# Cutting one product of each down chunk into two products of 256 columns

## The chip, the cores and the metric

The kernel runs on one core of one Trainium2 chip. The metric is the device time of one execution in microseconds (us). Before the change the median of 3 runs is 964.23 us (964.13 to 964.59).

## The reference

Two transformer-like blocks run one after the other on 256 tokens of width 1024, in fp32. Cut to what matters here:

```
x = x + rms_norm(mixer(rms_norm(x)))                        # attention of two kinds and a delta rule
u = conv3(rms_norm(x) @ w_up) + b                           # 1024 -> 2 * 2816
x = x + rms_norm((gelu(gate) * up) @ w_down)                # 2816 -> 1024
h = h + (u * spatial_gate(layernorm(v))) @ a_w_out          # 2048 -> 1024
h = h + square(relu(rms_norm(h) @ mlp_w1[0])) @ mlp_w2[0]   # 1024 -> 4096 -> 1024
h = h + latent_attention(rms_norm(h))
h = h + square(relu(rms_norm(h) @ mlp_w1[1])) @ mlp_w2[1]
out = rms_norm(h)
```

Four of these lines end in a product that comes "down" from a wide hidden vector to 1024 columns: `w_down`, `a_w_out`, and `mlp_w2` twice. The change touches these four.

## The kernel before, in words

**Products.** Every large fp32 product is done as three products of rounded operands (`fp32r`): each operand is split into a high part and a low part (`s0h`, `s0l` for a weight, `aT0h`, `aT0l` for an activation), and `mm3` (L456) issues high by high, high by low, low by high into the same PSUM bank. The first two of the three have the same stationary operand.

**Up and down.** `updown` (L553) runs each of the four stages. The weights come in chunks. An up chunk gives 256 hidden columns of all 256 tokens: `fm` (L462) does 16 groups of three products of 256 columns, with the weight as the stationary operand and the tokens as the moving one, into a bank named `r_fm`. After some work on ScalarE (ACT) and VectorE (DVE) the result is split into `aT`. A down chunk multiplies `aT` by 256 rows of the down weight: `down` (L486) goes over the two halves of the 1024 output columns, and `tm` (L469) over two blocks of 128 rows, each with three products of 512 columns, with `aT` as the stationary operand and the weight as the moving one. It is called for both blocks of 128 tokens (L599, L600), so a down chunk is 2 x 2 x 2 x 3 = 24 products of 512 columns, into four accumulators named `r_acc`. Up and down chunks alternate, the down chunk being 4 blocks behind the up chunk (`LAG`); in the first of the four stages two up chunks stand between two down chunks. The last 4 down chunks of a stage (`TAIL`) take another path for the second token block (`last_downs`, L620).

**Weights.** SyncE's queue (SP) loads each half chunk into one of four `raw` buffers (L324). ACT rounds it into a slot (`s2h<-raw`) and DVE subtracts (`s2l<-raw,s2h`). There are 4 to 6 slots; a slot is free when the last product that reads it is done. A `raw` buffer is free when DVE has read it, and the load after waits for that.

**Order.** The instruction order is not written out by hand. Threads (Python generators) offer their next instruction, and `run_threads` (L249) always takes the thread whose instruction would start first by the model in `Estimate` (L76); starts within 0.02 us are settled by rank, and a thread of rank 10 or more is put back by 0.3 us. Every instruction is one such choice, and a thread that comes to a free slot or a new event does so when its turn is taken. The model charges a product of n columns n/2400 us and 0.0023 us (L99). On the chip each engine then takes its own instructions strictly in the order that came out.

**Between the stages.** After the second stage, `latent_setup` (L1368) loads constants through the same SP queue, among them `inv_freq` into the tile `vm`, from which the thread `angles` (L1325) computes on DVE.

Of the kernel before, what the change touches and what calls it, by code (L numbers as in the profile page):

```python
# [21 lines left out]
TAIL = 4  # L22
# [22 lines left out]
def updown_plan(n, per=1):  # L45

    ev, nd = [], n // per
    for i in range(n):
        ev.append(("up", i))
        j = (i + 1) // per - 1 - LAG  # L50
        if (i + 1) % per == 0 and j >= 0:
            ev.append(("down", j))
    return ev + [("down", j) for j in range(nd - LAG, nd)]


def weight_plan():
    def stage(up, down, n, per=1):
        return [(up if k == "up" else down, i) for k, i in updown_plan(n, per)]

    seq = [("w_v", 0), ("w_v", 1)]  # L60
    seq += PROJ
    seq += [("w_z", 0), ("w_z", 1)]
    seq += [("w_out", i) for i in range(4)]
    seq += stage("w_up", "w_down", 22, 2)
    seq += [("a_v", i) for i in range(8)]
    seq += stage("a_u", "a_w_out", 8)
    seq += stage("w1_0", "w2_0", 16)
    seq += [("kv_a", 0), ("kv_a", 1), ("q_a", 0), ("q_a", 1)]
    seq += [("kv_b", 1), ("q_bp", 0), ("kv_b", 0), ("q_bn", 0), ("q_bn", 1)]
    seq += [("b_w_o", i) for i in range(4)]  # L70
    seq += stage("w1_1", "w2_1", 16)
    return seq
# [125 lines left out]
class Kernel:  # L198
# [254 lines left out]
            yield from self.T.transpose(dst[:, b * P:(b + 1) * P], src[:, b * P:(b + 1) * P], self.ident)  # L453


    def mm3(self, o, lh, ll, rh, rl, first, last):  # L456
        T = self.T
        yield from T.matmul(o, lh, rh, start=first, stop=False)
        yield from T.matmul(o, lh, rl, start=False, stop=False)
        yield from T.matmul(o, ll, rh, start=False, stop=last)  # L460

    def fm(self, o, w, c0, xT, nk):  # L462

# [2 lines left out]
            yield from self.mm3(o, w[0][:, k, c0:c0 + P], w[1][:, k, c0:c0 + P], xT[0][:, k, :], xT[1][:, k, :],  # L466
                     k == 0, k == nk - 1)

    def tm(self, o, w, xT, t, ks, k0=0, c0=0, n=None, first=True, last=True, ev=None):  # L469

        n = n or w[0].shape[2]
        ts = slice(t * P, (t + 1) * P)
        for i, k in enumerate(ks):
            yield from self.block_ready(w, k)
            if ev and (k0 + k) % 4 == 0:
                yield self.on((ev, t, (k0 + k) // 4))
            yield from self.mm3(o, xT[0][:, k0 + k, ts], xT[1][:, k0 + k, ts], w[0][:, k, c0:c0 + n], w[1][:, k, c0:c0 + n],
                     first and i == 0, last and i == len(ks) - 1)

    def new_acc(self, t):  # L480
        acc = []
# [1 line left out]
            acc.append((yield from self.bank("acc%d" % t)))  # L483
        return acc

    def down(self, acc, w, aT, t, k0, first, last):  # L486
        last = last if isinstance(last, tuple) else (last, last)
        for h in range(2):
            yield from self.tm(acc[h], w, aT, t, (0, 1), k0=k0, c0=h * 512, n=512, first=first, last=last[h])
            if last[h]:  # L490
                self.set(("sum", acc[h].name, 512 * h), acc[h])

# [60 lines left out]
    def updown(self, names, n, per, pool, block, aT, tail, stagger, gains=(), final=False):  # L553

        S, xT, nd = self.S, self.hT, n // per
        acc, st, last = None, {}, []

        def first(c):
            o = yield from self.bank("tp", st[0, c], st[1, c])
            for b in range(2):  # L560
                for t in range(2):
                    yield from self.T.transpose(o[:, b * 256 + t * P:b * 256 + (t + 1) * P], st[t, c][:, b * P:(b + 1) * P],
                                     self.ident)
            yield from block(c, o)

        if stagger:
            ws = []
            for t in range(2):
                for c in range(stagger):
                    if len(ws) <= c:  # L570
                        ws.append((yield from self.chunk(names[0], c)))
                    o = (yield from self.bank("fm"))[:, :256]
                    yield from self.tm(o, ws[c].view(8), xT, t, range(8), ev=names[0])
                    st[t, c] = self.tile(pool, [P, 256], "tmst", bufs=2 * stagger)
                    self.spawn(1, self.copy_out(st[t, c], o))
                    if t:
                        self.free(ws[c])
                        self.spawn(1, first(c))
        else:
            yield self.on((names[0], 0), (names[0], 1))  # L580
        for kind, i in updown_plan(n, per):
            if kind == "up":
                if stagger and i < stagger:
                    continue
                c = yield from self.chunk(names[0], i)
                o = yield from self.up(c.view(8), xT)
                self.free(c)
                self.spawn(1, block(i, o))
                if i == n // 2:
                    self.g = [self.gain(g) for g in gains]  # L590
                continue
            if acc is None:
                acc = [[], []]
                for t in range(2):
                    acc[t] = yield from self.new_acc(t)
            c = yield from self.chunk(names[1], i)
            yield self.on((names[0], "block", i))
            if i < nd - TAIL:
                yield from self.down(acc[0], c.view(2), aT[i], 0, 0, i == 0, False)  # L599
                yield from self.down(acc[1], c.view(2), aT[i], 1, 0, i == 0, (False, final and i == nd - TAIL - 1))  # L600
                self.free(c)
                self.rel(aT[i][0])
            else:
                yield from self.down(acc[0], c.view(2), aT[i], 0, 0, i == 0, i == nd - 1)
                last.append((i, c))
        for t in range(2):
            tail(t, acc[t])
        items = [(c, aT[i], 0) for i, c in last]
        if not final:
            yield from self.last_downs([(acc[1][h], HALVES[h]) for h in range(2)], items, False)  # L610
            return

        for _ in range(2):
            acc[1].append((yield from self.bank("fm")))
        self.set(("sum", "banks"))
        yield from self.last_downs([(acc[1][0], HALVES[0])], items, False)
        for q in range(2):
            yield from self.last_downs([(acc[1][2 + q][:, :256], slice(512 + 256 * q, 768 + 256 * q))], items, True)
# [1010 lines left out]
```

## Time and profile before

| | before |
|---|---|
| median of 3 runs | 964.23 us (964.13 to 964.59) |
| the profiled execution, its time | 963.24 us |
| the profiled execution, its span | 961.5 us |
| mean granted TensorE clock | 0.992 |
| TensorE (PE) busy | 939.2 us, 98% |
| VectorE busy | 648.4 us, 67% |
| ScalarE busy | 515.0 us, 54% |
| instructions | 16153, of them 6475 products and 6475 weight loads |

The profiled execution has 1.74 us more in its time than in its span. All instructions are issued from one helper line, L177, so groups are told apart by the tiles they write and read: `out<-in`, for a product the moving operand first and the stationary one second. A product's row begins when it enters the array and ends with its modelled drain, so rows of successive products overlap, and the distance of two starts is what a product costs in a stream.

### The profile page before, as it was taken

Reading aid. Unit: us, or ns where it says so; the run is one execution under the profiler, and the core shown is the slowest. Engines: PE = TensorE matmul, PEld = TensorE weight load, DVE = VectorE, ACT = ScalarE, POOL = GpSimd, SP = SyncE. Lnnn points to the kernel's source line nnn. Section 1 sums busy time; section 2 is a strip of 40 time slices with the busy share of each in tenths; the row PEclk is TensorE's granted clock in tenths of the full one; section 3 lists DMA queues with packets and bytes.
Section 4 is the critical chain, followed back from the end, with each engine's and each line's share of the span. In section 5 each row is a group of like instructions: output and inputs, shape, how many; then the busy total and the mean of one; then the engine's idle time right before and its main releaser. Section 6 shows DMA issues by size and latency. Waiting matters only on the chain.

```text
span 961.5 us, 16153 instructions
## 1 busy us (share of the span) xinstructions
PE 939.2 (98%) x6475; PEld 863.1 (90%) x6475; DVE 648.4 (67%) x1027; ACT 515.0 (54%) x853; POOL 24.9 (3%) x38
## 2 busy tenths in 40 slices
PE   7999999999999999999998999999999999999997
PEld 6899878899999989999988999998889899999986
DVE  5687776889687757697557765554678687555533
ACT  5664565767566546535445644444557575444421
POOL 0000000000000001000000000000110000000000
PEclk8999999999999999999999999999999999999999
DMA  7732432746777637727645776564345377566511
GB/s 230 252 111 89 132 110 88 223 132 197 254 227 233 201 113 287 244 88 259 193 133 152 244 226 192 192 194 148 96 149 161 111 231 240 186 202 194 193 47 44
DMA packets 48891, 168.22 MB, mean 175 GB/s; under 512 B 6448, under 2 KB 7088, under 8 KB 48560
## 3 DMA queue, kind: packets, MB, share of 16 engines
q1 hardware_dynamic: 48816, 167.19, 54.5%
q8 instruction: 51, 0.84, 0.4%
q14 instruction: 24, 0.20, 0.1%
HBM read 166.12 MB, written 1.05 MB: 174 GB/s over the span
## 4 chain that ended last, share of the span: by engine, by line
PE 90%; DVE 3%; ACT 2%; DMA 2%; issue 1%; SPq 1%; POOL 0%; POOLq 0%; DVEq 0%; ACTq 0%
PE r_fm L177 47%; PE r_acc L177 38%; PE r_tp L177 5%; DMA x<-x 1%; DMA vm<-inv_freq 1%; ACT junk L177 1%; DVE r_xg L177 1%; DVE cT L177 1%; DMA raw<-w_up 1%; DVE s4l L177 0%; POOL rstd L177 0%; DVE s3l L177 0%; DVE s0l L177 0%; DVE xTl L177 0%; ACT cT L177 0%
## 5 line engine op out<-in xcount | busy, mean ns | idle before, releaser
L177 DVE TENSOR_TENSOR s0l<-raw,s0h 128x1024 fp32r<-128x1024 f32 (+1 forms) x54 | 64.8, 1211 | 19.8 <-ACT s0h L177 19.7
L177 DVE TENSOR_TENSOR s2l<-raw,s2h 128x1024 fp32r<-128x1024 f32 (+1 forms) x54 | 65.1, 1212 | 17.4 <-ACT s2h L177 17.2
L177 DVE TENSOR_TENSOR s3l<-raw,s3h 128x1024 fp32r<-128x1024 f32 (+1 forms) x56 | 66.8, 1201 | 14.9 <-ACT s3h L177 14.7
L177 DVE TENSOR_TENSOR s1l<-raw,s1h 128x1024 fp32r<-128x1024 f32 (+2 forms) x54 | 64.8, 1201 | 15.5 <-ACT s1h L177 15.2
L177 ACT ACTIVATE s0h<-raw 128x1024 fp32r<-128x1024 f32 (+1 forms) x54 | 55.6, 1046 | 26.4 <-PE r_acc L177 17.2
L177 PE MATMUL r_fm<-xTh,s1h 128*128 128x256 f32 x240 | 67.3, 280 | 0.0
L177 PE MATMUL r_fm<-xTl,s1h 128*128 128x256 f32 x240 | 67.3, 280 | 0.0
L177 PE MATMUL r_fm<-xTh,s1l 128*128 128x256 f32 x240 | 67.3, 280 | 0.0
L177 DVE TENSOR_TENSOR s4l<-raw,s4h 128x1024 fp32r<-128x1024 f32 (+1 forms) x46 | 55.2, 1210 | 16.7 <-ACT s4h L177 16.7
L177 ACT ACTIVATE s3h<-raw 128x1024 fp32r<-128x1024 f32 (+1 forms) x56 | 57.5, 1036 | 16.8 <-PE r_acc L177 10.2
L177 ACT ACTIVATE s2h<-raw 128x1024 fp32r<-128x1024 f32 (+1 forms) x54 | 56.0, 1045 | 16.7 <-PE r_acc L177 9.7
L177 DVE TENSOR_TENSOR r_q<-r_r 128x512 f32<-128x512 f32 x32 | 22.1, 692 | 62.1 <-ACT r_r L177 62.0
L177 ACT ACTIVATE s1h<-raw 128x1024 fp32r<-128x1024 f32 (+2 forms) x54 | 55.9, 1037 | 14.4 <-DMA raw<-w_up 5.3
L177 ACT ACTIVATE r_r<-r_fm 128x512 f32<-128x512 f32 x26 | 15.6, 599 | 80.5 <-PE r_fm L177 80.5
L177 ACT ACTIVATE s4h<-raw 128x1024 fp32r<-128x1024 f32 (+1 forms) x46 | 47.4, 1043 | 18.8 <-PE r_acc L177 9.8
L177 PE MATMUL r_fm<-xTh,s3h 128*128 128x256 f32 x200 | 56.3, 281 | 0.4 <-DVE cT L177 0.4
L177 PE MATMUL r_fm<-xTl,s3h 128*128 128x256 f32 x200 | 56.2, 281 | 0.0
L177 PE MATMUL r_fm<-xTh,s3l 128*128 128x256 f32 x200 | 56.1, 281 | 0.0
L177 PE MATMUL r_fm<-xTl,s2h 128*128 128x256 f32 x176 | 49.4, 281 | 0.0
L177 PE MATMUL r_fm<-xTh,s2l 128*128 128x256 f32 x176 | 49.4, 280 | 0.0
L177 PE MATMUL r_fm<-xTh,s2h 128*128 128x256 f32 x176 | 49.3, 280 | 0.0
L177 POOL TENSOR_TENSOR rstd<-rstd,mhalf 128x1 f32<-128x1 f32 (+1 forms) x30 | 23.9, 798 | 931.4 <-DVE rstd L177 914.7
(611 smaller groups left out, 3153.8 us busy)
## 6 DMA issues: line engine op xcount, KB each, us to landing
raw<-w SPq DMA_DIRECT2D x128, 512.0 KB, 4.6
raw<-w_up SPq DMA_DIRECT2D x44, 512.0 KB, 4.8
raw<-w_down SPq DMA_DIRECT2D x22, 512.0 KB, 4.9
raw<-a_v SPq DMA_DIRECT2D x16, 512.0 KB, 5.6
raw<-a_u SPq DMA_DIRECT2D x16, 512.0 KB, 4.5
raw<-a_w_out SPq DMA_DIRECT2D x16, 512.0 KB, 4.7
raw<-w_c SPq DMA_DIRECT2D x12, 512.0 KB, 5.2
raw<-w_out SPq DMA_DIRECT2D x8, 512.0 KB, 3.7
```

What stands on the lines that cost most here:

```text
L177: f(*args, **kw)
```

## The change

The third product of the last group of three (low by high) of the second token block's second output half is issued as two products of 256 columns, with the same stationary operand and the two halves of the same moving operand, into the two halves of the same bank. All other products stay as they are.

```
-    def mm3(self, o, lh, ll, rh, rl, first, last):
+    def mm3(self, o, lh, ll, rh, rl, first, last, cut=None):
         T = self.T
         yield from T.matmul(o, lh, rh, start=first, stop=False)
         yield from T.matmul(o, lh, rl, start=False, stop=False)
-        yield from T.matmul(o, ll, rh, start=False, stop=last)
+        parts = (slice(0, cut), slice(cut, None)) if cut else (slice(None),)
+        for c in parts:
+            yield from T.matmul(o[:, c], ll, rh[:, c], start=False, stop=last and c is parts[-1])
...
             yield from self.mm3(o, xT[0][:, k0 + k, ts], xT[1][:, k0 + k, ts], w[0][:, k, c0:c0 + n], w[1][:, k, c0:c0 + n],
-                     first and i == 0, last and i == len(ks) - 1)
+                     first and i == 0, last and i == len(ks) - 1, cut if i == len(ks) - 1 else None)
...
             if i < nd - TAIL:
                 yield from self.down(acc[0], c.view(2), aT[i], 0, 0, i == 0, False)
-                yield from self.down(acc[1], c.view(2), aT[i], 1, 0, i == 0, (False, final and i == nd - TAIL - 1))
+                yield from self.down(acc[1], c.view(2), aT[i], 1, 0, i == 0, (False, final and i == nd - TAIL - 1),
+                                     cut=256)
                 self.free(c)
```

`tm` and `down` only hand the argument on; `down` gives it to its second half alone. The branch is taken for down chunks other than the last 4 of a stage. The stages have 11, 8, 16 and 16 down chunks, so it is taken 7, 4, 12 and 12 times: 35 products become 70.

## Rows read from the trace of the kernel before

**Rows 1.** From the page: busy time of TensorE, and the chain that ended last, by engine and by line.
```profile
PE 939.2 (98%) x6475; PEld 863.1 (90%) x6475; DVE 648.4 (67%) x1027; ACT 515.0 (54%) x853; POOL 24.9 (3%) x38
...
PE 90%; DVE 3%; ACT 2%; DMA 2%; issue 1%; SPq 1%; POOL 0%; POOLq 0%; DVEq 0%; ACTq 0%
```

**Rows 2.** Busy time of each engine in five stretches: the first stage's steady part, the second's, the junction after it, and the two MLPs' steady parts. Columns: stretch, its length, busy us of PE, PEld, DVE, ACT and POOL (instructions), the granted clock, the DMA engines' share, GB/s.
```profile
201.00:333.00 132.00, 132.00 (x1000) 126.37 (x999) 107.29 (x163) 82.63 (x124) 0.00 (x0) 1.00 0.65 208
436.00:476.00 40.00, 40.00 (x274) 36.99 (x273) 25.29 (x27) 20.18 (x24) 0.00 (x0) 1.00 0.73 238
476.00:531.00 55.00, 51.80 (x321) 46.90 (x320) 35.43 (x62) 25.83 (x40) 1.10 (x2) 0.97 0.48 140
531.00:661.00 130.00, 130.00 (x863) 119.63 (x862) 76.71 (x77) 64.27 (x77) 0.00 (x0) 1.00 0.65 205
800.00:927.00 127.00, 127.00 (x838) 116.71 (x837) 70.33 (x71) 58.12 (x70) 0.00 (x0) 1.00 0.59 187
```

**Rows 3.** The chain in order of time (start us, us, what): a down chunk and the two up chunks after it in the first stage; a down chunk, an up chunk and the next down chunk in the first MLP; and the last products of the kernel, 48 of them with 256 columns and `aT` as the stationary operand.
```profile
232.58 5.46 PE r_acc L177 x24
238.03 11.31 PE r_fm L177 x96
...
605.20 5.44 PE r_acc L177 x24
610.64 5.65 PE r_fm L177 x48
616.29 5.44 PE r_acc L177 x24
...
948.98 5.76 PE r_fm L177 x48
```

**Rows 4.** TensorE's instructions in order of time where a down chunk ends and an up chunk begins (start us, us, engine, line, operation, out<-in). The second row is a product that the change cuts.
```profile
610.02 0.39 PE L177 MATMUL r_acc<-s2l,r_aT1h 128*128 128x512 f32 x1
610.25 0.39 PE L177 MATMUL r_acc<-s2h,aT1l 128*128 128x512 f32 x1
610.48 0.28 PE L177 MATMUL r_fm<-xTh,s3h 128*128 128x256 f32 x1
610.59 0.28 PE L177 MATMUL r_fm<-xTl,s3h 128*128 128x256 f32 x1
610.71 0.28 PE L177 MATMUL r_fm<-xTh,s3l 128*128 128x256 f32 x1
```

**Rows 5.** Weight loads (PEld) by group in the up chunk from 610.64 to 616.29 us, one of the groups: busy us, mean ns of one.
```profile
L177 PEld LDWEIGHTS r_fm<-xTh,s3l 128*128 128x128 f32 x16 | 3.1, 192 | 0.0
```

**Rows 6.** What follows on the other engines when that down chunk ends, from the timelines of ACT, DVE and PE: the freed slot is filled, and its next reader.
```profile
610.67 2.01 ACT L177 ACTIVATE s2h<-raw 128x1024 fp32r<-128x1024 f32 x2 [2.37 <-PE r_acc L177]
...
611.77 2.36 DVE L177 TENSOR_TENSOR s2l<-raw,s2h 128x1024 fp32r<-128x1024 f32 x2 [1.93 <-ACT s2h L177]
...
638.32 0.39 PE L177 MATMUL r_acc<-s2h,r_aT4h 128*128 128x512 f32 x1
```

**Rows 7.** TensorE's timeline in the second stage: work of another thread (`c_wsT`) between the products of a down chunk.
```profile
450.82 0.39 PE L177 MATMUL r_acc<-s4h,aT1l 128*128 128x512 f32 x1
451.05 1.05 PE L177 MATMUL r_tp<-c_wsT,v 128*128 128x128 f32 x8
451.86 0.48 PE L177 MATMUL r_acc<-s4h,r_aT1h 128*128 128x512 f32 x1
```

**Rows 8.** The junction after the second stage: first the chain in order of time, then the timelines of DVE, POOL, SP and PE, and last the stretch from 514 to 516 us in the columns of rows 2.
```profile
500.18 1.14 DVE s0l L177
...
501.33 0.33 SPq L324
...
504.08 6.98 DMA vm<-inv_freq
...
514.03 7.39 PE r_fm L177 x52
...
502.87 1.22 DVE L177 TENSOR_TENSOR s0l<-raw,s0h 128x1024 fp32r<-128x1024 f32 x1
...
511.16 0.24 DVE L177 TENSOR_SCALAR vm<-vm 128x32 f32<-128x32 f32 x1 [4.15 <-DMA vm<-inv_freq]
511.31 1.41 DVE L177 SCALAR_TENSOR_TENSOR r_xg<-x,rstd,gb 128x512 f32<-128x512 f32 x2
...
507.01 0.55 POOL L177 TENSOR_TENSOR rstd<-rstd,mhalf 128x1 f32<-128x1 f32 x1 [12.70 <-DVE vm L177]
...
496.92 4.74 SPq L324 DMA_DIRECT2D raw<-w  x3
501.76 0.38 SPq L288 DMA_DIRECT2D c_mla_flags<-mla_flags  x1
...
512.21 0.63 PE L177 MATMUL r_tp<-c_ident,r_xg 128*128 128x128 f32 x4 [3.20 <-DVE r_xg L177]
512.59 0.36 PE L177 MATMUL r_fm<-s4l,xTh 128*128 128x256 f32 x1
...
515.11 0.41 PE L177 MATMUL r_fm<-s0h,xTl 128*128 128x256 f32 x1
515.32 0.41 PE L177 MATMUL r_fm<-s0h,xTh 128*128 128x256 f32 x1
...
514.00:516.00 2.00, 2.00 (x12) 2.00 (x11) 1.90 (x8) 0.60 (x1) 0.00 (x0) 0.50 0.41 96
```

More of the change, by code (lines that the diff above doesn't have):

```diff
@@ L467, in fm, with tm @@
                      k == 0, k == nk - 1)
-    def tm(self, o, w, xT, t, ks, k0=0, c0=0, n=None, first=True, last=True, ev=None):
+    def tm(self, o, w, xT, t, ks, k0=0, c0=0, n=None, first=True, last=True, ev=None, cut=None):
         n = n or w[0].shape[2]
@@ L484, in new_acc, with down @@
         return acc
-    def down(self, acc, w, aT, t, k0, first, last):
+    def down(self, acc, w, aT, t, k0, first, last, cut=None):
         last = last if isinstance(last, tuple) else (last, last)
         for h in range(2):
-            yield from self.tm(acc[h], w, aT, t, (0, 1), k0=k0, c0=h * 512, n=512, first=first, last=last[h])
+            yield from self.tm(acc[h], w, aT, t, (0, 1), k0=k0, c0=h * 512, n=512, first=first, last=last[h],
+                               cut=cut if h else None)
             if last[h]:
```

## The prediction

> **What bounds the kernel now.** I read four views, in this order. The page says that the chain that ended last is TensorE for 90% of the span, and TensorE is busy for 98% of it [rows 1]. So a product that becomes longer is paid for wherever nothing else is late. The busy time by stretch shows where that is: in the stretches of the first stage and of both MLPs TensorE is busy for every microsecond at the full granted clock of 1.00, while DVE and ACT have 19% and more to spare; only the junction after the second stage has TensorE idle, with the clock at 0.97 in the mean [rows 2]. The reader is to see there that 31 of the 35 cuts (7, 12 and 12) stand in stretches where TensorE alone sets the pace, and the other 4 in the second stage, which is also full (40.00 of 40.00 us).
>
> The chain in order of time then gives the pace itself: 24 products of 512 columns take 5.44 us and 48 of 256 columns take 5.65 us, and the pieces touch each other, 605.20 + 5.44 = 610.64 and 610.64 + 5.65 = 616.29 [rows 3]. One product thus costs 5.44/24 = 226.7 ns or 5.65/48 = 117.7 ns. And TensorE's own timeline at the seam answers whether the last product of a down chunk is followed by a stall that a shorter one could shrink: it starts at 610.25 and the first product of the up chunk at 610.48, 0.23 us later, the same as from the 512-column product before it (610.02 to 610.25, 0.23) [rows 4]. There is nothing to win at the seam.
>
> **The change part by part.** *The products.* Removed: 35 products of 512 columns, 226.7 ns each. Added: 70 of 256 columns. Their price is read from the stream that is most like them. In an up chunk, two products of 256 columns with the same stationary operand follow each other (610.48 and 610.59, both with `s3h`) and the next, with another one, comes at 610.71 [rows 4]; the mean over the chunk is 117.7 ns [rows 3]. So one cut costs 2 x 117.7 - 226.7 = 8.7 ns, and 35 cuts 0.31 us. Every one of them is on the path, since TensorE has no gap there to hide it. The upper bound comes from the last 48 products of the kernel, which have 256 columns and `aT` as the stationary operand like the new halves: 5.76/48 = 120.0 ns [rows 3], so 2 x 120.0 - 226.7 = 13.3 ns a cut and 0.47 us in all. The lower bound is 0: the same 512 columns pass, and the seam has no stall to give back. I take 8.7 ns, because the halves stand between products of an up chunk and a down chunk in a stage where the 117.7 ns were measured.
>
> *The added weight loads.* Each new half brings a load of its own, 35 more. The load's row lasts 192 ns [rows 5], longer than a 256-column product's place in the stream, and still 48 products with 48 loads pass in 5.65 us [rows 3]; the loads run beside the products before them, and 117.7 ns already contains what they cost. The Trainium skill, in "TensorE: Matmul & The Clock Gate", section "Part 3: Packing small matmuls — row/col tiling", says that a load overlaps a running product only where the two use different row groups, and its section "LDWEIGHTS (loading the stationary operand)" prices a load of 128 columns at about 107 ns; all products here are 128 rows deep, so by that rule the change would cost an estimated 35 x 107 ns = 3.7 us. By that rule the trace does not agree: 48 loads of 107 ns and 48 products of 107 ns one after the other would be over 10 us, and the row says 5.65.
>
> *The end of the chunk.* The slot and the `aT` buffer are released by the last product. The cut product begins at 610.25 and ends by the model 0.39 us later, at 610.64; ACT starts to fill the freed slot at 610.67 [rows 4, 6]. The second half would begin 0.12 us after the first, at 610.37, and last 0.28 us: 610.65. The release moves by about 0.01 us. What waits for it, ACT's rounding and DVE's subtraction, ends at 611.77 + 2.36 = 614.13, and that slot is next read at 638.32 [rows 6]: 24 us of cover. ACT has been idle for 2.37 us before the release, so nothing queued behind it is late either. SP's loads follow DVE's reads, so they move by the same 0.01 us.
>
> *The order.* This part no row can settle. The order comes from a model, and the change gives that model one more choice per cut and adds 2 x (256/2400 + 0.0023) - (512/2400 + 0.0023) = 0.0023 us to its clock, 11 x 0.0023 = 0.025 us by the end of the second stage and 0.08 us over all 35. The steps that follow the cut (the freed chunk, the next chunk's claim) also take their turn half a product later. Other threads' work does slip in between products, as the 8 products of `c_wsT` between two products of a down chunk [rows 7], but that is work whose turn comes from its own operands and not at the last product. In the steady stages there is no other thread with work for TensorE or it is far from the cut, so an exchange on ACT or DVE there is covered by their idle time. Where all threads hang on TensorE's clock, they all move by the same 0.0023 us and no choice turns over; it takes a near tie. I count it at 0 in the sum, and it makes the rivals.
>
> *The sum.* On the profiled execution: span 961.5 + 0.31, with 1.74 us around it, so 963.24 + 0.31 = 963.55 us. The median of the runs stands 0.99 us above the profiled execution, so in its terms 964.23 + 0.31 = 964.5 us, +0.03%. About 0.2%, 1.9 us, is what a measurement of this kernel can tell from no change.
>
> **The rivals.** *Faster: the model's order at the junction turns over.* At 511.16 DVE starts an instruction on `vm` that has waited 4.15 us for the load of `inv_freq`; behind it in DVE's queue stands `r_xg`, whose other operand POOL had finished at 507.01 + 0.55 = 507.56. TensorE waits 3.20 us for `r_xg`, and afterwards runs at 1.2 GHz for a while (granted clock 0.50 from 514 to 516, 256-column products 0.21 us apart) [rows 8]. If `r_xg` came first, its first transposes could start as now 512.21 - 511.31 = 0.90 us after it, at about 508.5, before TensorE has run dry. The price is 3.20 us and what the low clock cost: 52 products took 7.39 us against 52 x 0.1177 = 6.12, so 1.27. Together 4.5 us: 960.0 us. For it: it is the largest stall that one exchange of two instructions would remove. Against: it must turn over by a shift of some 0.025 us, and the two instructions are not seen to be near a tie.
>
> *Slower: SP's queue at the same junction takes one more weight load before the constants.* Three `raw` loads stand before them; the last could go only when DVE's `s0l` ended at 501.32, then come the constants, and `inv_freq` lands at 511.06 [rows 8]. The next `raw` buffer is free when the second `s0l` ends, 502.87 + 1.22 = 504.09. If the order put that one load first, the constants would go 504.09 - 501.32 = 2.8 us later, DVE's wait and TensorE's would grow by as much, and the time would be 964.5 + 2.8 = 967.3 us. It decides from the first additional load on. For it: the constants are issued when the main thread passes the last product of the stage, the loads when the splitter takes its turn, so the two orders are a race in the model. Against: there is no cut in the last 4 chunks, so only the common shift reaches this place.
>
> *Slower: the weight load of the second half is not covered.* By the load's row, 35 x 192 ns [rows 5] is 6.7 us: 971 us. Against it stands every up chunk.
>
> *The change does not do what it says.* If the two halves were issued as one, or the branch not taken, the time would be 964.2 us. The branch is the steady path of all four stages, so this is only a matter of a few tenths within my forecast.
>
> **How the numbers follow.** The forecast, including exchanges in the order that cost or give less than 1.9 us, has 0.74; the exchange at the junction or another like it that gives more, 0.14; the queue's order or another exchange that costs more, 0.10; uncovered loads, 0.02. So faster 0.14, same 0.74, slower 0.12. The forecast's own range is 962.3 (1.9 us below 964.2) to 966.2. To that I add the queue's case with a little room, to 967.5, which holds some 0.84; the gain of 4.5 us is left out.
>
> **What would show it.** In the trace after: 7, 4, 12 and 12 pairs of `r_acc` products of 256 columns at the ends of down chunks, 6510 products in all; the second of a pair 0.12 us after the first, and the up chunk's first product 0.12 us after that; the steady down chunk 5.45 us and no longer 5.44; the clock unchanged; the junction with its wait for `inv_freq` of about 4.2 us in the same place. Wrong would be a pair that takes more than 0.25 us, which is the case of the loads, or a junction where DVE's wait has another length or another instruction behind it, which is the case of the order; then the difference of the two traces up to 476 us would still be some 0.1 us, and all the rest would lie after it.

## The result, and the profile after

The changed kernel takes 959.08 us (median of 5 runs, 957.23 to 961.72) against 964.13 us before (5 runs, 963.34 to 964.59): ratio 0.9949, 95% interval 0.9931 to 0.9966. It is faster by about 0.5%, outside the range, and on the side that had been given 0.14. Two later series of the same kernel, on two chips, gave 0.9924 (0.9904 to 0.9945) and 0.9928 (0.9913 to 0.9943).

First the page of the kernel after: busy time, and the chain that ended last by engine.

```profile
PE 936.3 (98%) x6510; PEld 860.7 (90%) x6510; DVE 648.6 (68%) x1027; ACT 514.4 (54%) x853; POOL 24.9 (3%) x38
...
PE 88%; DVE 4%; ACT 3%; DMA 3%; issue 1%; SPq 1%; POOL 0%; POOLq 0%; DVEq 0%; ACTq 0%
```

There are 35 products more, as forecast, and TensorE is busy for 2.9 us less [rows 1]. So the time was not won by removing a wait; the products themselves got shorter. Which ones, the chain in order of time of the kernel after shows (start us, us, what); these pieces answer to rows 3.

```profile
203.42 32.98 PE r_fm L177 x280
236.40 5.45 PE r_acc L177 x25
241.84 10.90 PE r_fm L177 x96
...
539.63 5.46 PE r_acc L177 x25
...
605.15 5.46 PE r_acc L177 x25
610.61 5.46 PE r_fm L177 x48
...
659.75 20.91 PE r_acc L177 x93
...
804.70 5.46 PE r_acc L177 x25
...
924.82 21.81 PE r_acc L177 x97
```

The reader is to see that the cut chunk hardly changed (5.44 to 5.46 us), while the up chunk behind it, in which nothing was edited, fell from 5.65 to 5.46 us, and the two up chunks of the first stage from 11.31 to 10.90. A product of 256 columns there now takes 5.46/48 = 113.8 ns, where it took 117.7. It is not the clock: the granted clock of the first MLP's steady part is 1.00 before [rows 2] and after:

```profile
531.00:661.00 130.00, 130.00 (x887) 119.73 (x886) 77.68 (x79) 66.07 (x79) 0.00 (x0) 1.00 0.65 208
```

TensorE's timeline at the seam of the kernel after (the place of rows 4; `x2` is the cut pair):

```profile
609.99 0.39 PE L177 MATMUL r_acc<-s2l,r_aT1h 128*128 128x512 f32 x1
610.21 0.40 PE L177 MATMUL r_acc<-s2h,aT1l 128*128 128x256 f32 x2
610.45 0.29 PE L177 MATMUL r_fm<-xTh,s3h 128*128 128x256 f32 x1
610.57 0.28 PE L177 MATMUL r_fm<-xTl,s3h 128*128 128x256 f32 x1
610.69 0.28 PE L177 MATMUL r_fm<-xTh,s3l 128*128 128x256 f32 x1
610.80 0.28 PE L177 MATMUL r_fm<-xTh,s3h 128*128 128x256 f32 x1
```

The pair and the first two products of the up chunk come 0.12 us apart; further on the distance falls, and over the chunk the mean is 113.8 ns. What I had named as the places of other mechanisms is unchanged. The release of the slot and the wait for `inv_freq` stand in the timelines of ACT and DVE of the kernel after:

```profile
610.65 1.06 ACT L177 ACTIVATE s2h<-raw 128x1024 fp32r<-128x1024 f32 x1 [2.39 <-PE r_acc L177]
...
512.14 0.24 DVE L177 TENSOR_SCALAR vm<-vm 128x32 f32<-128x32 f32 x1 [4.12 <-DMA vm<-inv_freq]
```

The wait of 4.15 us [rows 8] is still 4.12 us with the same instruction behind it. A list of the instructions of both kernels engine by engine differs in the 35 products with their weight loads and in nothing else, so the order did not turn over anywhere.

**Where the time went.** The stretches of the two chains can be subtracted; these are the pieces of the chain before at which they begin and end:

```profile
538.62 5.45 PE r_acc L177 x24
...
660.66 20.86 PE r_acc L177 x92
...
805.18 5.46 PE r_acc L177 x24
...
927.23 21.76 PE r_acc L177 x96
```

From the first MLP's first down chunk to its last downs: 122.04 us before (538.62 to 660.66), 120.12 after (539.63 to 659.75), -1.92. The second MLP: 122.05 (805.18 to 927.23) and 120.12 (804.70 to 924.82), -1.93. From the first stage's first down chunk to the first MLP's: 306.04 (232.58 to 538.62) and 303.23 (236.40 to 539.63), -2.81. Together -6.66 us. The sum by chunks comes to nearly the same: 22 up chunks in the MLPs, 3 in the second stage and 6 pairs in the first follow a cut, 25 x 0.19 + 6 x 0.41 = 7.2 us, less 35 x 0.02 = 0.7 us for the cuts, 6.5 us.

The profiled execution of the kernel after shows only 961.5 - 959.1 = 2.4 us of it, because its start up to the first down chunk took 236.40 us instead of 232.58, 3.82 us more, and the part between the two MLPs (660.66 to 805.18, 659.75 to 804.70) 0.43 us more. No instruction was changed before the first down chunk. Busy time, granted clock and DMA in one stretch of this start (columns as in rows 2), before:

```profile
40.00:42.00 2.00, 2.00 (x21) 2.00 (x20) 1.66 (x3) 1.25 (x2) 0.00 (x0) 1.00 0.81 214
```

and after:

```profile
40.00:42.00 2.00, 2.00 (x11) 2.00 (x11) 1.22 (x1) 1.69 (x2) 0.00 (x0) 0.50 0.66 152
```

After a gap of TensorE from 34.32 us on (2.35 us before, 2.78 after, `issue` in the chain) the clock fell to 1.2 GHz in the second execution and not in the first, and by 44 us the difference was 2.0 us. Another 1.23 us is in the stream of 280 products before the first down chunk, 31.75 us before against 32.98. Both vary between executions of one kernel. In the two later profiled executions of the changed kernel the granted clock stayed at 1.00 there, and the stream of 280 took, in the one and in the other:

```profile
200.66 31.75 PE r_fm L177 x280
...
201.04 32.98 PE r_fm L177 x280
```

### The profile page after: what moved, and what is told of

Same layout as the page of the kernel before. It is cut to its first block, busy times and chain, and to the rows that moved or that the text cites. A ratio compares the mean times of both kernels' runs of the same rounds, so it can differ in the third digit from the quotient of the medians.

```text
span 959.1 us, 16223 instructions
## 1 busy us (share of the span) xinstructions
PE 936.3 (98%) x6510; PEld 860.7 (90%) x6510; DVE 648.6 (68%) x1027; ACT 514.4 (54%) x853; POOL 24.9 (3%) x38
## 4 chain that ended last, share of the span: by engine, by line
PE 88%; DVE 4%; ACT 3%; DMA 3%; issue 1%; SPq 1%; POOL 0%; POOLq 0%; DVEq 0%; ACTq 0%
PE r_fm L177 45%; PE r_acc L177 38%; PE r_tp L177 5%; DMA x<-x 1%; DMA vm<-inv_freq 1%; ACT junk L177 1%; DMA raw<-w_up 1%; DVE cT L177 1%; DVE r_xg L177 1%; DMA raw<-w 1%; DVE xTl L177 0%; DVE s4l L177 0%; DVE s3l L177 0%; DVE r_cv L177 0%; ACT s2h L177 0%
## 5 line engine op out<-in xcount | busy, mean ns | idle before, releaser
L177 DVE TENSOR_TENSOR s0l<-raw,s0h 128x1024 fp32r<-128x1024 f32 (+1 forms) x54 | 64.7, 1211 | 21.1 <-ACT s0h L177 20.9
L177 DVE TENSOR_TENSOR s3l<-raw,s3h 128x1024 fp32r<-128x1024 f32 (+1 forms) x56 | 66.8, 1202 | 16.4 <-ACT s3h L177 16.4
L177 DVE TENSOR_TENSOR s2l<-raw,s2h 128x1024 fp32r<-128x1024 f32 (+1 forms) x54 | 65.1, 1212 | 18.0 <-ACT s2h L177 17.8
L177 DVE TENSOR_TENSOR s1l<-raw,s1h 128x1024 fp32r<-128x1024 f32 (+2 forms) x54 | 64.7, 1202 | 15.8 <-ACT s1h L177 15.6
L177 ACT ACTIVATE s0h<-raw 128x1024 fp32r<-128x1024 f32 (+1 forms) x54 | 55.6, 1046 | 29.0 <-PE r_acc L177 17.3
L177 ACT ACTIVATE s3h<-raw 128x1024 fp32r<-128x1024 f32 (+1 forms) x56 | 57.5, 1036 | 18.6 <-PE r_acc L177 10.2
L177 PE MATMUL r_fm<-xTh,s1h 128*128 128x256 f32 x240 | 66.7, 278 | 0.0
L177 PE MATMUL r_fm<-xTl,s1h 128*128 128x256 f32 x240 | 66.7, 278 | 0.0
L177 PE MATMUL r_fm<-xTh,s1l 128*128 128x256 f32 x240 | 66.7, 278 | 0.0
L177 ACT ACTIVATE s2h<-raw 128x1024 fp32r<-128x1024 f32 (+1 forms) x54 | 56.1, 1045 | 17.7 <-PE r_acc L177 7.3
L177 DVE TENSOR_TENSOR s4l<-raw,s4h 128x1024 fp32r<-128x1024 f32 (+1 forms) x46 | 55.2, 1210 | 15.0 <-ACT s4h L177 14.8
L177 ACT ACTIVATE s1h<-raw 128x1024 fp32r<-128x1024 f32 (+2 forms) x54 | 56.0, 1038 | 13.9 <-DMA raw<-w_up 5.2
L177 DVE TENSOR_TENSOR r_q<-r_r 128x512 f32<-128x512 f32 x32 | 22.1, 692 | 58.6 <-ACT r_r L177 58.5
L177 ACT ACTIVATE r_r<-r_fm 128x512 f32<-128x512 f32 x26 | 15.5, 597 | 77.2 <-PE r_fm L177 77.2
L177 PE MATMUL r_fm<-xTh,s3h 128*128 128x256 f32 x200 | 55.8, 279 | 0.4 <-DVE cT L177 0.4
L177 ACT ACTIVATE s4h<-raw 128x1024 fp32r<-128x1024 f32 (+1 forms) x46 | 47.4, 1043 | 16.2 <-PE r_acc L177 8.4
L177 PE MATMUL r_fm<-xTl,s3h 128*128 128x256 f32 x200 | 55.7, 279 | 0.0
L177 PE MATMUL r_fm<-xTh,s3l 128*128 128x256 f32 x200 | 55.6, 278 | 0.0
L177 PE MATMUL r_fm<-xTl,s2h 128*128 128x256 f32 x176 | 49.0, 278 | 0.0
L177 PE MATMUL r_fm<-xTh,s2h 128*128 128x256 f32 x176 | 49.0, 278 | 0.0
L177 PE MATMUL r_fm<-xTh,s2l 128*128 128x256 f32 x176 | 49.0, 278 | 0.0
L177 POOL TENSOR_TENSOR rstd<-rstd,mhalf 128x1 f32<-128x1 f32 (+1 forms) x30 | 23.9, 797 | 929.0 <-DVE rstd L177 912.4
```

Of the source, the lines that this page charges most:

```text
L177: f(*args, **kw)
```

## The experiments

Theory P, formed from the two traces: TensorE has two spacings for a stream of 256-column products, 117.7 and 113.7 ns, and each keeps itself; a settled stream of 512-column products leads into the slow one, and a product of another length shortly before the seam leads into the fast one. Its rivals: more products or another instruction layout as such, the order of the weight loads, and the exact lengths. In none of the runs did the instruction order of any engine change otherwise than by the edit.

**What must stand at the seam.** Four kernels keep the number of products of the change and move or reshape the cut. Where lines of `mm3` are shown, the line that makes `parts` moves ahead of them or is left out.

The cut in the first product:

```
-        yield from T.matmul(o, lh, rh, start=first, stop=False)
+        for c in parts:
+            yield from T.matmul(o[:, c], lh, rh[:, c], start=first, stop=False)
         yield from T.matmul(o, lh, rl, start=False, stop=False)
-        for c in parts:
-            yield from T.matmul(o[:, c], ll, rh[:, c], start=False, stop=last and c is parts[-1])
+        yield from T.matmul(o, ll, rh, start=False, stop=last)
```

Other lengths, 384 and 128 columns in one kernel (the diff) and 128 and 384 in the other (`cut=128`):

```
-                                     cut=256)
+                                     cut=384)
```

The halves apart:

```
         yield from T.matmul(o, lh, rh, start=first, stop=False)
+        if cut:
+            yield from T.matmul(o[:, :cut], ll, rh[:, :cut], start=False, stop=False)
         yield from T.matmul(o, lh, rl, start=False, stop=False)
-        for c in parts:
-            yield from T.matmul(o[:, c], ll, rh[:, c], start=False, stop=last and c is parts[-1])
+        c = parts[-1]
+        yield from T.matmul(o[:, c], ll, rh[:, c], start=False, stop=last)
```

> The first product of the last group of three is cut instead of the third, so the up chunk again follows a product of 512 columns; number and kind of instructions as in the changed kernel. Theory A (what stands directly before an up chunk sets the spacing of its 48 products: 117.7 ns after a product of 512 columns, 113.7 ns after a cut one): up chunks of the MLPs 5.65 us as before the change, down chunks about 5.46 us, time 964.1 + 35 x 0.02 = 964.8 us. Theory B (35 more instructions anywhere, or another place of the instructions, bring the gain): up chunks 5.46 us, time about 959 us.

> The third product is cut into 384 and 128 columns. Theory A1 (any break of the 512-column rhythm at the seam changes the spacing): up chunks about 5.46 us, time within 1 us of 959. Theory A2 (the fast spacing needs a 256-column product ahead, the same length as those of the up chunk): up chunks 5.65 us, time about 965 us, since the 128-column piece takes about 111 ns like the transposes and brings nothing.

> The third product is cut into 128 and 384 columns, so a longer product than 256 columns is the last. A1: up chunks about 5.46 us, time within 1 us of 959. A2: up chunks 5.65 us, about 965 us. Theory A3 (the seam needs two successive products with one stationary operand, of whatever length): up chunks 5.46 us here and in the run with 384 and 128 columns.

> The two halves are kept but stand apart: high by high (512 columns), low by high first half, high by low (512), low by high second half. One 256-column product stands before the up chunk, with no other product of its stationary operand next to it. A2 (a 256-column product ahead is enough): up chunks 5.46 us, time about 959 us. A3 (two in succession with one stationary operand are needed): up chunks 5.65 us, time about 964.8 us.

Measured, ratio to the kernel before on the same chip (median 966.66 us): cut first 958.16 us, 0.9913 (0.9888 to 0.9939); 384 and 128 959.49, 0.9934 (0.9914 to 0.9954); 128 and 384 960.57, 0.9948 (0.9921 to 0.9975); halves apart 957.31, 0.9906 (0.988 to 0.9932). All four are faster. The chain in order of time of the kernel with the cut in the first product:

```profile
558.66 5.48 PE r_acc L177 x25
564.14 5.46 PE r_fm L177 x48
```

of the one with 384 and 128 columns:

```profile
556.46 5.51 PE r_fm L177 x48
561.98 5.46 PE r_acc L177 x25
```

and of the one with 128 and 384:

```profile
554.41 5.47 PE r_fm L177 x48
559.88 5.51 PE r_acc L177 x25
```

With the halves apart, the up chunks take 5.46 us too; their first distances stand in the list further below.

Theories A2 (a 256-column product must be ahead) and A3 (two with one stationary operand must follow each other) fall, by the run with 384 columns last and by the halves apart. Theory A falls in its narrow form: two whole products may stand between the cut and the seam. What was left: any break (A1), or simply more products (B).

**How far from the seam, and whether more products are enough.** Two kernels move the same cut away, with three and with six products of 512 columns between it and the up chunk.

Six between (in `down`), then three between (in `tm`):

```
-                               cut=cut if h else None)
+                               cut=None if h else cut)
```

```
-                     first and i == 0, last and i == len(ks) - 1, cut if i == len(ks) - 1 else None)
+                     first and i == 0, last and i == len(ks) - 1, cut if i == 0 else None)
```

> The same cut, but in the second token block's first output half, so that six products of 512 columns stand between it and the up chunk. Theory P (TensorE's stream of 256-column products has two spacings that keep themselves, 117.7 and 113.7 ns; a settled stream of 512-column products always leads into the slow one, and a disturbance shortly before the seam leads into the fast one; after a seam in the changed kernel the 512-column products took 231, 233 and 231 ns and then 227 again, so a disturbance is forgotten after some 3 to 5 products): up chunks of the MLPs 5.65 us, ratio to the kernel before 1.000 to 1.001. Theory B (35 more products anywhere in the down chunks bring the gain): up chunks 5.46 us, ratio about 0.993.

> The cut is in the first group of the last half instead of the second, so three products of 512 columns stand between it and the up chunk. Theory P: with two between, the products took 234 and 235 ns and the up chunk became fast; with six between they took 233, 235, 229, 233, 231, 227 and it stayed slow. The third is at 229 and not yet settled at 227, so the up chunk should become fast: 5.46 us, ratio about 0.993. If what counts is only whether the cut is in the group right before the seam: 5.65 us, ratio 1.001.

Six between: 965.58 us (before 964.22 on the same chip), ratio 1.0011 (0.9998 to 1.0024). Three between: 967.57 us (before 965.03), ratio 1.0025 (1.0014 to 1.0037). The chain of the first:

```profile
558.95 5.65 PE r_fm L177 x48
564.60 5.47 PE r_acc L177 x25
```

and of the second:

```profile
552.79 5.51 PE r_acc L177 x25
558.30 5.65 PE r_fm L177 x48
```

The same 35 cuts bring nothing as soon as they are too early, so theory B falls, and the distance decides. My expectation for three between was wrong: I had taken it for the condition that the 512-column stream is not yet settled when the up chunk begins, and that does not hold (see the list below). That kernel pays the cuts alone, 35 x (5.51 - 5.44) = 2.4 us, which is its ratio.

**Whether the order of the weight loads is disturbance enough.** Nothing is cut in these two. Both change the order of the three products from high by high, high by low, low by high as below, the one in the group that the change cuts, the other in the first group of every up chunk.

```
         yield from T.matmul(o, lh, rh, start=first, stop=False)
-        yield from T.matmul(o, lh, rl, start=False, stop=False)
-        yield from T.matmul(o, ll, rh, start=False, stop=last)
+        yield from T.matmul(o, ll, rh, start=False, stop=False)
+        yield from T.matmul(o, lh, rl, start=False, stop=last)
```

> Nothing is cut; in the group that the change cuts the order is high by high, low by high, high by low, so the stationary operands alternate there. P1 (another order of the weight loads is disturbance enough): up chunks 5.46 us, ratio about 0.993, and a little better than the change since no product is added. P2 (only a product of another length disturbs): up chunks 5.65 us, ratio 1.000.

> Nothing is cut; the first group of three of every up chunk is done in the order high by high, low by high, high by low, inside the stream of 256-column products. P1: the spacing falls from 117.7 to 113.7 ns after the first products of the chunk, up chunks about 5.47 us, ratio about 0.993. P2: up chunks 5.65 us, ratio 1.000.

Swap in the down chunk: 965.41 us, ratio 1.0001 (0.9987 to 1.0015). Swap in the up chunk: 964.81 us, ratio 1.0001 (0.9986 to 1.0016). The chain of the first:

```profile
555.01 5.44 PE r_acc L177 x24
560.45 5.65 PE r_fm L177 x48
```

P2 holds at these two places: the sequence of stationary operands alone moves nothing, and a product of another length does. Over all profiled executions this is without exception: the 31 seams from a steady down chunk to an up chunk lead into the fast spacing in each of the nine executions with a cut at most two products ahead, and into the slow one in each of the five others.

**The distances themselves.** The trace keeps starts to the nanosecond. This list, worked out from them for one seam of the first MLP in each kernel, gives the columns of the last nine products before the up chunk with the time to the next start in ns, and behind the bar those times for the first nine products of the up chunk.

```
before        512:227 512:227 512:226 512:227 512:227 512:226 512:227 512:227 512:226 | 118 117 119 117 118 118 117 118 118
after         512:227 512:227 512:226 512:227 512:227 512:226 512:227 256:113 256:120 | 120 122 116 114 113 114 113 113 114
cut first     512:226 512:227 512:227 512:226 512:227 256:113 256:120 512:233 512:236 | 116 118 119 116 114 113 114 113 113
384, 128      512:227 512:226 512:227 512:227 512:226 512:227 512:227 384:170 128:60  | 170 117 123 118 113 114 113 113 114
128, 384      512:226 512:227 512:227 512:226 512:227 512:227 512:226 128:58  384:228 | 118 116 118 122 119 113 113 114 113
halves apart  512:226 512:227 512:227 512:226 512:227 512:227 256:113 512:232 256:118 | 123 119 113 113 114 113 113 114 113
three between 512:226 512:227 512:227 512:226 256:114 256:119 512:233 512:236 512:228 | 117 117 118 118 118 117 119 117 118
six between   512:227 256:114 256:118 512:233 512:237 512:227 512:233 512:231 512:227 | 118 116 120 117 118 117 118 118 118
swap down     512:226 512:227 512:227 512:226 512:227 512:227 512:226 512:227 512:227 | 117 118 118 118 117 118 118 117 119
swap up       512:227 512:227 512:226 512:227 512:227 512:226 512:227 512:227 512:226 | 118 117 119 117 118 118 117 118 118
```

The settled 512-column stream repeats 226 and 227 and leads into 117 to 119 without a transient. After a cut the distances are uneven for a few products (233, 236, 232). Where the up chunk begins at most two products behind the cut, it goes through 116 to 123 (once 170, behind the piece of 128 columns) and then stays at 113 and 114 to its end. Unevenness as such is not the condition: in the row of six between, the fourth and fifth product behind the cut are again at 233 and 231, so with three between the up chunk also begins while the stream is uneven, and it is slow.

**Whether other slow streams can be tipped, and whether another version beats the change.** One kernel adds two cuts inside streams and leaves out the 4 cuts that no up chunk follows; another adds the seams of two tails; the change itself ran beside them, and once before.

With `fm` and `up` handing a cut on to the last group of the first 128 columns of a chunk, as `tm` does, the first of them is:

```
-                o = yield from self.up(c.view(8), xT)
+                o = yield from self.up(c.view(8), xT, cut=128 if names[0] == "w_up" and i == stagger else None)
...
-                                     cut=256)
+                                     cut=256 if i < nd - TAIL - 1 else None)
...
-            yield from self.tm(o, w.view(8), hT, t, range(8), ev="a_v")
+            yield from self.tm(o, w.view(8), hT, t, range(8), ev="a_v", cut=128 if t == 1 and c == 0 else None)
```

The second has besides, with 256 given in the first stage's tail and in the end of the kernel:

```
-                                   first=fresh and m == 0, last=m == len(items) - 1)
+                                   first=fresh and m == 0, last=m == len(items) - 1,
+                                   cut=cut if m == len(items) - 1 and o is parts[-1][0] else None)
```

> The changed kernel with the cut left out where no up chunk follows (the last one of each stage, 4 of 35), and with one product cut into two of 128 columns inside two streams that are still slow: near the start of the second stage's stream from about 373 to 410 us (spacing 117.8 ns in every trace so far), and in the first up chunk after the first stage's start (the stream of 280 products that took 31.75 or 32.98 us). Theory P (any product of another length tips a stream of 256-column products into the fast spacing, where it stays): the first gains about 280 x 4.0 ns less some 0.1 us for the added product, the second takes about 31.8 us in the profile; together 1 to 2 us less than the changed kernel. Rival (only the seam from 512 to 256 columns matters): both streams as before, the time that of the changed kernel within 0.3 us.

> As the run with more cuts in slow streams, and two more seams cut: the last product of 512 columns before the second stage's first stream (78 products at 117.8 ns), and the one before the last 48 products of the kernel (120.0 ns each). Theory P: the 78 products at 113.7, 0.3 us less; for the last 48, whose stationary operand is the activation, P says nothing of a faster spacing: 5.76 us stays or falls to 5.46. The time 0 to 0.5 us below that of the other run.

> The changed kernel once more, on the same chip as the other runs of this call, to see how far single executions lie apart and whether the up chunks always take 5.46 us. Theory P: 5.46 us in the MLPs again, since the seam is the same in every chunk, and what differs between executions lies before the first cut (the first stage's stream of 280 products took 31.75 us in one execution and 32.98 in another).

> The changed kernel on the same chip, as the measure for the two runs beside it. Theory P: up chunks 5.46 us in the MLPs, ratio to the kernel before 0.992 to 0.995.

Measured: more cuts inside streams 958.82 us, 0.9933 (0.992 to 0.9946); with the tails 957.96, 0.9926 (0.991 to 0.9942); the change beside them 958.16, 0.9928 (0.9913 to 0.9943), and in the earlier series 957.79, 0.9924 (0.9904 to 0.9945). In both its series the changed kernel's up chunks took 5.46 us. None of the further cuts beats it beyond the interval; nor do the halves apart, whose interval overlaps those of the change. The cut inside a stream (a kick) worked in the first stage in the one execution where it was needed: in the kernel with the tails it came in a stream at 117 to 119 ns, and 114 was reached six products later; that stream's chain piece:

```profile
201.85 31.94 PE r_fm L177 x281
```

The kick in the second stage did nothing. The timeline of the first of the two kernels there:

```profile
374.04 0.33 PE L177 MATMUL r_fm<-s4h,xTl 128*128 128x128 f32 x2
374.21 0.34 PE L177 MATMUL r_fm<-s0h,xTh 128*128 128x256 f32 x1
374.38 0.28 PE L177 MATMUL r_fm<-s0l,xTh 128*128 128x256 f32 x1
374.50 0.28 PE L177 MATMUL r_fm<-s0h,xTl 128*128 128x256 f32 x1
374.62 0.28 PE L177 MATMUL r_fm<-s0h,xTh 128*128 128x256 f32 x1
```

It stays at 0.12 us, and so do the streams behind the tails; the chain of the kernel with the tails:

```profile
360.11 9.19 PE r_fm L177 x78
...
943.30 5.77 PE r_fm L177 x48
```

They took 9.19 us (`361.22 9.19 PE r_fm L177 x78` in its chain) and 5.76 us [rows 3] before. So P as I wrote it (any product of another length tips any stream of 256-column products) is too wide.

In these three streams the activation is the stationary operand and the weight the moving one, the other way round than in an up chunk. That alone does not explain it, since the trace of before has short streams of this kind in the fast spacing, here one behind transposes, the first and the last of 25 products on end:

```profile
190.65 0.28 PE L177 MATMUL r_fm<-s3h,xTl 128*128 128x256 f32 x1
...
193.37 0.28 PE L177 MATMUL r_fm<-s5h,xTl 128*128 128x256 f32 x1
```

24 distances in 2.72 us are 113.3 ns each; 13 of the 14 profiled executions have such a stream. Nor is a product of another length the only thing that tips a stream. The slow stream of the second stage passes into one with the weight as the stationary operand, with 256 columns on both sides, and that one is fast in all 14 executions; before:

```profile
407.05 0.28 PE L177 MATMUL r_fm<-s1h,xTl 128*128 128x256 f32 x1
407.17 0.29 PE L177 MATMUL r_fm<-xTh,s2h 128*128 128x256 f32 x1
407.29 0.28 PE L177 MATMUL r_fm<-xTl,s2h 128*128 128x256 f32 x1
407.41 0.28 PE L177 MATMUL r_fm<-xTh,s2l 128*128 128x256 f32 x1
...
408.09 0.28 PE L177 MATMUL r_fm<-xTh,s2l 128*128 128x256 f32 x1
```

From 407.41 on six distances take 0.68 us, 113.3 ns each. And products of 128 columns ahead do not always lead into the fast spacing: the first stage's stream of 280 stands behind transposes of 128 columns, and without a kick it was fast in 5 executions and slow in 7, twice slow and once fast with the changed kernel itself. So what is shown is the effect of a cut close ahead of an up chunk, and not a rule for every stream.

## Why the prediction was wrong

*What bounds the kernel* was right: TensorE alone sets the pace where the cuts are, and each ns of a product there is a ns of the run.

*"There is nothing to win at the seam"* is the step that failed. I looked for a stall at the seam, found 0.23 us like any other distance, and took the spacing behind it for the price of a 256-column product. It is the price of one state of the stream. The lower bound of 0 fell with it: I had argued that the same columns pass, and left out the 48 or 96 products behind the cut. Their term was put at nothing, and the runs show 0.19 us less for each up chunk and 0.41 us less for each pair of them, 7.2 us over the 31 seams. The signs that I had named for a wrong forecast did not appear (the pair takes 0.23 us and not more than 0.25, and the wait at the junction is unchanged), so they could not have told it. The trace of before could have. Two pieces of its chain:

```profile
200.82 31.75 PE r_fm L177 x280
...
254.78 11.31 PE r_fm L177 x96
```

These are products of the same kind in the same stage, 31.75/280 = 113.4 ns each in the one and 11.31/96 = 117.8 ns in the other. I used the second price and never asked why the first was lower.

*The cost of the cut* was right at the cut and too low for the chunk: the pair takes 113 + 120 = 233 ns instead of 227, against 8.7 ns forecast and 13.3 as the upper bound, but the chunk takes 5.46 - 5.44 = 0.02 us more. The rest is in the down chunk's first three products, which take 231 to 233 ns behind a fast up chunk instead of 227. Where no gain covers it, the cut costs 0.07 us a chunk with three products between and 0.03 us with six.

*The added weight loads* were right: they are hidden. The rule of the Trainium skill ("TensorE: Matmul & The Clock Gate", section "Part 3: Packing small matmuls — row/col tiling") that a load overlaps a running product only in another row group does not agree with these traces either: 48 loads and 48 products now pass in 5.46 us, even less than before.

*The release at the end of the chunk* was right: ACT starts to fill the slot 0.42 us after the start of the product that is cut before (610.25 to 610.67) and 0.44 us after (610.21 to 610.65), and is idle until then in both.

*The order* was right in the sum and wrong as the main rival. It did not turn over in any of the kernels, and the chance of a gain had been hung on it. The gain came by a mechanism that was on no list; that the side on which it fell had been given 0.14 is luck. *The queue of SP* and *uncovered loads* did not come about.

## What to carry to other kernels

When one kind of instruction in a back-to-back stream has two spacings in different places of one trace, its price is a state of the stream, and an edit just ahead of a long stream is to be priced over the whole stream: here 0.02 us a cut paid for 0.19 to 0.41 us behind it. Compare the time per product of equal pieces across the whole chain before taking one of them for the price. And compare stage by stage: the profiled execution showed 2.4 us of a gain of 6.7, since its start, where nothing was changed, took 3.8 us longer.

## What was not expected of the hardware

- A stream of `fp32r` products of 256 columns runs at one of two spacings, 117.7 ns a product or 113.7 in the mean of a fast up chunk (113.3 where it has settled), for 48, 96 and 280 products on end, at a granted clock of 1.00 in both.
- Directly after a settled stream of 512-column products (226.7 ns) an up chunk was slow in every execution without a cut; with a product of 128, 256 or 384 columns at most two products ahead it was fast; with three or six of 512 columns between, slow again.
- Behind transposes of 128 columns the same stream of 280 products was fast in one execution and slow in another (31.75 and 32.98 us), and a change of the stationary operand from activation to weight tipped a stream without any change of length.
- With the activation as the stationary operand the spacing was 113.3, 117.8 or 120.0 ns. In the three streams where it was tried, neither a cut inside the stream nor one ahead of it changed 117.8 and 120.0.
- What in TensorE holds the two states was not found. The order of the weight loads does not (two runs), nor does their number (six between). In the slow up chunk the loads of the low part take 192 ns [rows 5], in the fast one (610.61 to 616.07 us) 188 like the others; whether that is cause or effect is open. A bare pause of TensorE ahead of an up chunk, and the reading of the operands, were not tried.
